# Regrouping the logit steps of the first attention in a two-layer encoder

## The chip, the core and the metric

The kernel runs on one core of a Trainium2 chip. A core has five engines that take their instructions from queues of their own, in order: TensorE (PE in the profile, with its weight loads as PEld), VectorE (DVE), ScalarE (ACT), GpSimd (POOL) and SyncE (SP, which here starts the transfers). Matmul results land in PSUM, from which VectorE and ScalarE read them into SBUF. The metric is the device time of one execution in microseconds (us), lower is better. The time before is a median of three runs.

## The reference

A sequence of 512 tokens of width 1024 goes through two layers. Each layer has a token mixer and, beside it, an attention of four heads into 256 memory tokens; their outputs are joined, projected and added to the stream, and a gated MLP with a short convolution follows. The change lies in the first layer, whose token mixer is the differential attention: six heads, each with two sets of queries and keys of 64 columns (`m` = 0, 1) and one set of values of 128 columns. Cut to what matters:

```python
q = rms_norm(q, qk_norm_g[0]) * (d ** -0.5)          # d = 64
k = rms_norm(k, qk_norm_g[1])
# for each block of 128 queries:
logits = einsum('bhmqd,bhmkd->bhmqk', qb, k) + bias  # two sets of logits a head
logits = where(key_chunk <= query_chunk, logits, -inf)
p = softmax(logits)
w = p[:, :, 0] - lam * p[:, :, 1]
o = rms_norm(einsum('bhqk,bhkv->bhqv', w, v), out_norm_g) * (1.0 - lam_init)

# memory attention, 4 heads of 64 columns:
o_mem = softmax(rms_norm(q_mem) * 64 ** -0.5 @ rms_norm(k_mem).T) @ v_mem

x = x + concatenate([o, o_mem]) @ w_out
x = x + conv_ffn(rms_norm(x), ...)
```

## The kernel before

**Matmuls of weights.** Weights and activations are split into a high and a low part (ScalarE's copy at L253 and VectorE's subtraction at L256 for weights; L310 and L311, the function `split`, for activations), and each product is made of three matmuls, high by high, low by high and high by low: `gemm` (L330 to L332) for projections, `product` (L351 to L353) for the output projection. These are full matmuls: 128 rows, 512 columns.

**The first attention.** The blocks of queries of a pair of heads are worked off in five steps. `TOGETHER` says which blocks (head, block) share a step, so that each step has up to 512 columns of keys:

```python
TOGETHER = (((0, 2), (0, 0)), ((0, 3),), ((0, 1), (1, 1)), ((1, 2), (1, 0)), ((1, 3),))
```

Three pairs of heads give steps 0 to 14. A step passes through three functions. `logits(t)` issues 6, 4, 8, 6 or 4 matmuls (for the five steps of a pair; the trace shows each as two, 12, 8, 16, 12 and 8), whose keys and queries have 64 rows only; the two sets `m` go to the upper and the lower half of the array and to two PSUM banks. VectorE then adds the bias and takes the row's extreme (L726), ScalarE takes the exponential (L729), and VectorE forms the weights `w`. `turn(t)` transposes them into a bank "tp" (L220), which ScalarE copies out (L748). `values(t)` multiplies them by the values into a bank "sm"; after the last block of a head, `output` squares the result on ScalarE (L771), `scale` normalises it on VectorE (L777, L779), and `finish` transposes it through a bank "tp" and splits it with L310 and L311. `prepare(h)` makes the queries and keys of a head: eight transposes through both banks "tp", each emptied by ScalarE (L682).

The memory attention has the same structure: `queries` (two banks "tp", L582), `logits` of a block of 128 queries (L591; 64 rows as well), `softmax` (L599 and L605 to L607 on VectorE, L603 on ScalarE), `turn` and `values`. The method `logits` takes any number of blocks: the first uses the banks "lg", a second one "tp" in the first layer and "sm" in the second, where two blocks are issued together. The memory's keys and values are made in `operands` and `keys` (L310, L551, L552, L560).

**PSUM.** There are four tags, "mm", "lg", "sm" and "tp", of two banks each (`bank`, L193). Banks of a tag are used in turn: who asks for one waits until its last reader is through.

**Order.** TensorE's order is that of the program (`manual_schedule`); the order of the other engines is the scheduler's. Through the first attention the program is read from a string, `SCRIPT`, by `do` (L633). A letter with a number calls a function, by the table `doing`: `L` is logits, `M` logits with the banks "tp" (in the table, but not used by this script), `T` turn, `V` values, `P` prepare, `N` the norms of queries and keys, `F` finish, `s` scale, `a` and `b` the memory operands of the two layers, `k` memory keys, `q` the memory queries (`q0` their norm, `q1` their transposes), `l`, `t`, `v` logits, turn and values of the memory attention, `X` the loads of the residual stream, `O` the last part of the output projection. A plain number is filler, in us by the program's own reckoning: `Filler.fill` takes full matmuls of the projections from a queue (six at a time for 512 columns) or of the output projection (three at a time, reckoned at 0.65) until the number is used up. In the trace the script's stretch lies between about 48 and 217 us.

The residual update (L1061, in `update`) reads the output projection's banks, "mm" among them, on VectorE.

Of the kernel before, what the change touches and what calls it, by code (L numbers as in the profile page):

```python
# [37 lines left out]

SCRIPT = """
    17.75 P0 3.9  # L40
    L0 a3 P1 8.45 a0 0.97
    L1 1.94 a1 T0
    L2 3.57 a2
    L3 T1 4.86 N2 V0 T2 N3 V1 12.33
    L4 P2 6.17 V2 T3
    L5 s0 T4 2.27 V3
    L6 P3 b1 V4 5.2 T5
    L7 T6 F0 7.14 b0
    L8 V5 T7 8.42 V6 s1 N5 N4 F1
    L9 V7 P4 b2 4.45 T8 T9 s2 3.0  # L50
    L10 V8 3.55 X P5 q0
    L11 b3 V9 T10 4.2
    L12 F2 V10 s3 T11 3.8 q1 k0
    L13 3.15 l0 V11 T12 3.65
    L14 F3 t0 3.3 V12 T13 t1 l1 3.9 T14 l2 t2 2.3 O k1 t3 s4 l3 v0 t4 V13 V14 t6 t5 1.3 t7 F4 v1 s5 F5 6.15 ! 4.55
"""

ORDER = (('v', 0), ('qk', 1), ('kv', 0), ('qk', 2), ('vm', 2), ('kv', 1))
# [28 lines left out]
def _pieces():  # L87

    plan = []

    def piece(key, name, i, ks, *ranges):
        plan.append((key, name, i, ks, ranges))

    for l in range(2):
        if l == 0:
            w = "w_in_diff"
            piece(("qk", 0), w, 0, K8, (0, 256), (768, 1024))
            for key in ORDER:
                if key[0] == "qk":
                    p = key[1]  # L100
                    piece(key, w, 0, K8, (256 * p, 256 * p + 256), (768 + 256 * p, 1024 + 256 * p))
                elif key[0] == "kv":
                    piece(key, "w_mem_kv", key[1], K8, (0, 512))
                elif key[0] == "vm":
                    p = key[1]
                    piece(key, w, 0, K8, (1536 + 256 * p, 1792 + 256 * p), (2304, 2560))
                else:
                    p = key[1]
                    piece(key, w, 0, K8, (1536 + 256 * p, 2048 + 256 * p))
        else:  # L110
            w = "w_in_gla"
            piece(("gm", 1), w, 0, K8, (2304, 2576))
            for c in range(5):
                piece(("g", c), w, 0, K8, (512 * c, min(512 * c + 512, 2304)))
        for i, part in enumerate(PASS[l]):
            for c, ks in part:
                piece(("o", l, i, c), "w_out", l, ks, (256 * c, 256 * c + 256))
        base = 0
        for nq in HALVES:
            for q in range(base, base + nq):  # L120
                piece(("ua", l, q), "w_up", l, K8, (256 * q, 256 * q + 256))
                piece(("ug", l, q), "w_up", l, K8, (DFF + 256 * q, DFF + 256 * q + 256))
            for c in range(4):
                piece(("dn", l, base, c), "w_down", l, tuple(range(2 * base, 2 * base + 2 * nq)),
                      (256 * c, 256 * c + 256))
            base += nq
    return plan


def _blocks():  # L130

    out = []
    for key, name, i, ks, ranges in _pieces():
        w = sum(b - a for a, b in ranges)
        step = WTILE // w
        out.append([(name, i, ks[j:j + step], ranges, w) for j in range(0, len(ks), step)])
    return out
# [42 lines left out]
def trunk(ctx, tc, head_d, x_t, mem_t, wpack, cols_a_d, cols_d, conv_d, gate_d, rel_bias, diff_lambda, consts, onehot, out):  # L180
# [12 lines left out]
    def bank(tag):  # L193
        return ps.tile([128, 512], F32, name=f"ps_{tag}", tag=tag)

    def xtile():
        return xs.tile([128, S], F32, name="xt", tag="xs", bufs=XS)
# [9 lines left out]
    def blk(b, w=128):  # L207
        return slice(w * b, w * b + w)
# [40 lines left out]
    plan, blocks, made = _pieces(), _blocks(), []  # L249
# [318 lines left out]
    class MemAttn:  # L568
# [13 lines left out]
                A.activation(self.qT[hp], p, AF.Copy, scale=c_mq(self.l))  # L582


        def logits(self, *blocks):
            banks = [(bank(tag), bank(tag)) for _, tag in zip(blocks, ("lg", "sm") if self.l else ("lg", "tp"))]
            for b, pl in zip(blocks, banks):
                for hp in range(2):
                    for j in range(2):
                        hh = blk(j, 64)  # L590
                        mm(pl[j][:, blk(hp, 256)], self.qT[hp][hh, blk(b)], kmT[self.l][hh, hp], start=True, stop=True)  # L591
            for b, pl in zip(blocks, banks):
                self.softmax(b, pl)
# [51 lines left out]
    def diff_layer(pool, mix, acc):  # L645
# [45 lines left out]
        def members(t):  # L691
            pr, s = divmod(t, len(TOGETHER))
            out, at = [], 0
            for j, i in TOGETHER[s]:
                out.append((2 * pr + j, i, 4 * j + i, at))
                at += 128 * (i + 1)
            return pr, out, at

        def bias(h):
            bt = heads[h]["bt"] = pool.tile([128, S], F32, name="bt", bufs=2)  # L700
            src = bass.AP(tensor=bias_d.tensor, offset=bias_d[h].offset + 1, ap=[[1, 128], [1, 512]])
            nc.sync.dma_start(bt, src)
            G.memset(bt[0:64, 0:64], -1e30)

        def logits(t, tag="lg"):
            pr, group, _ = members(t)
            P = pairs[pr]
            s2, nm, rc = P["s2"], P["nm"], P["rc"]
            for h, _, _, _ in group:
                if "bt" not in heads[h]:  # L710
                    bias(h)
            pls = bank(tag), bank(tag)
            for h, i, _, at in group:
                nk = 128 * (i + 1)
                cuts = (0, nk) if i == 0 else (0, nk // 2, nk)
                for k0, k1 in zip(cuts, cuts[1:]):
                    for m in range(2):
                        hh = blk(m, 64)
                        mm(pls[m][:, at + k0:at + k1], heads[h]["q"][hh, blk(i)], heads[h]["k"][hh, k0:k1],
                           start=True, stop=True)  # L720
            e = xtile(), xtile()
            for m in range(2):
                for h, i, g, at in group:
                    c = slice(at, at + 128 * (i + 1))
                    n1 = nm[:, 8 * m + g:8 * m + g + 1]
                    V.tensor_tensor_reduce(  # L726
                        out=e[m][:, c], in0=pls[m][:, c], in1=heads[h]["bt"][:, 127 + 128 * i::-1], scale=-1.0,
                        scalar=1e38, op0=ALU.add, op1=ALU.min, accum_out=n1)
                    A.activation(e[m][:, c], e[m][:, c], AF.Exp, scale=-1.0, bias=n1,  # L729
                                              accum_out=s2[:, m, g:g + 1])  # L730
            ids = sorted(g for _, _, g, _ in group)
            step = max(ids[-1] - ids[0], 1)
            b, lr = slice(ids[0], ids[-1] + 1, step), slice(8 + ids[0], 9 + ids[-1], step)
            V.reciprocal(rc[:, b], s2[:, 1, b])
            V.scalar_tensor_tensor(rc[:, lr], rc[:, b], nlam, s2[:, 0, b], op0=ALU.mult, op1=ALU.mult)
            for _, i, g, at in group:
                c = slice(at, at + 128 * (i + 1))
                V.scalar_tensor_tensor(e[1][:, c], e[1][:, c], rc[:, 8 + g:9 + g], e[0][:, c],
                                                    op0=ALU.mult, op1=ALU.add)
            live[t] = e[1]  # L740
# [57 lines left out]
        ma = MemAttn(pool, 0, qm, mix, False)  # L798
        ops, keys = [None] * 2, [None] * 2
        for key in ORDER:  # L800
# [16 lines left out]

        doing = {
            "L": logits, "M": lambda i: logits(i, "tp"), "T": turn, "V": values, "P": prepare, "F": finish,
            "N": lambda i: norms(i // 2, i % 2), "a": lambda i: ops[0]((2 * i, 2 * i + 1)),  # L820
            "b": lambda i: ops[1]((2 * i, 2 * i + 1)), "k": lambda i: keys[i]("sm"),
            "q": lambda i: ma.queries() if i else (F.need("v2"), ma.norm()),
            "l": lambda i: ma.logits(i), "t": ma.turn, "v": lambda i: ma.values(i, "sm"),
            "s": lambda i: scales.pop(i)(), "X": lambda i: load_x(x_t),
            "O": lambda i: last.append(out_proj(0, mix, 1, acc, 5)), "!": lambda i: F.flush()}
        do(SCRIPT, doing)
# [228 lines left out]
    def load_x(src):  # L1055
        for k in range(KT):
            xT[k] = xtile()
            nc.sync.dma_start(xT[k], src[k])
# [117 lines left out]
    for l in range(2):  # L1176
        with tc.tile_pool(name=f"at{l}", bufs=2) as pool:
            mix = [None] * 8
            sums, acc = acc, [None]
            if l == 0:  # L1180
                diff_layer(pool, mix, acc)
            else:
                gla_layer(pool, mix, sums)
                out_proj(1, mix, len(PASS[1]) - 1, acc)
                F.flush()
        with tc.tile_pool(name=f"ff{l}", bufs=2) as pool:
            acc = ffn(pool, l, acc)
# [73 lines left out]
```

## Time and profile before

| | us |
|---|---|
| time, median of 3 runs | 1168.63 (1167.96 to 1169.76) |
| time of the profiled execution | 1168.01 |
| span of the profiled execution | 1166.2 |
| PE busy | 1160.7 (100%) |
| PEld busy | 965.3 (83%) |
| DVE busy | 750.9 (64%) |
| ACT busy | 545.5 (47%) |
| POOL busy | 5.0 (0%) |

The span runs from the first to the last instruction that the profiler recorded; the time of the execution also takes in what lies around it. Busy times of different engines overlap. An engine that is busy all the time can still be shortened, since a matmul that waits for the array to change its shape counts as busy. The throttle granted TensorE its full clock (1.0) in this execution.

### The profile page before, as it was taken

To read this page: it belongs to the slowest core of one execution; us is meant where nothing else is said; L and a number is where in the kernel's file an instruction comes from. 1 tells how busy PE (TensorE), PEld (TensorE's weight loads), DVE (VectorE), ACT (ScalarE), POOL (GpSimd) and SP (SyncE) were. 2 spreads that over 40 slices of the span, in tenths; PEclk is the share of its full clock that TensorE was granted. 3 is DMA by queue.
4 is the path that set the end of the run, shared out by engine and by line. 5 is a ranking of instruction groups with operands and counts; after the bars stand their busy time and mean duration, and the time that the engine had idled before them with its cause. 6 is when DMAs were issued, how large, how long until landed. Compare 5 with 4: busy or idle time off the path is not lost.

```text
span 1166.2 us, 14790 instructions
## 1 busy us (share of the span) xinstructions
PE 1160.7 (100%) x5658; PEld 965.3 (83%) x5658; DVE 750.9 (64%) x1256; ACT 545.5 (47%) x951; POOL 5.0 (0%) x27
## 2 busy tenths in 40 slices
PE   9999999999999999999999999999999999999998
PEld 7888888888888888888888888988888888888887
DVE  7576778688677326677447637777876743576741
ACT  6676687555344213344437634436643421343420
POOL 0000000000000000000000000000000000000000
PEclk9999999999999999999999999999999999999999
DMA  8423242123223223222342230333232323232231
GB/s 295 158 70 99 78 141 73 63 103 130 85 90 120 83 88 124 75 91 98 120 148 68 81 108 3 110 121 109 93 123 73 98 102 108 85 114 73 89 101 45
DMA packets 39556, 117.68 MB, mean 101 GB/s; under 512 B 4703, under 2 KB 7192, under 8 KB 39486
## 3 DMA queue, kind: packets, MB, share of 16 engines
q1 hardware_dynamic: 39054, 116.35, 29.5%
q8 instruction: 44, 0.72, 0.3%
q10 hardware_dynamic: 432, 0.39, 0.1%
q14 instruction: 26, 0.21, 0.1%
HBM read 112.52 MB, written 4.21 MB: 100 GB/s over the span
## 4 chain that ended last, share of the span: by engine, by line
PE 98%; ACT 1%; DVE 1%; issue 0%; POOL 0%; DVEq 0%; POOLq 0%
PE ps_mm L352 9%; PE ps_mm L351 9%; PE ps_mm L353 9%; PE ps_sm L353 8%; PE ps_sm L352 8%; PE ps_sm L351 7%; PE ps_mm L330 6%; PE ps_mm L332 6%; PE ps_mm L331 6%; PE ps_tp L353 3%; PE ps_lg L353 3%; PE ps_lg L352 3%; PE ps_tp L352 3%; PE ps_lg L351 3%; PE ps_tp L351 3%; PE ps_tp L220 3%
## 5 line engine op out<-in xcount | busy, mean ns | idle before, releaser
L253 ACT CAST whi<-raw 128x1024 fp32r<-128x1024 f32 (+4 forms) x212 | 207.6, 986 | 245.4 <-PE ps_tp L352 120.9
L256 DVE TENSOR_TENSOR wlo<-raw,whi 128x1024 fp32r<-128x1024 f32 (+4 forms) x212 | 240.3, 1140 | 117.5 <-ACT whi L253 116.6
L351 PE MATMUL ps_mm<-xsh,whi 128*128 128x512 f32 x438 | 171.6, 392 | 0.0
L352 PE MATMUL ps_mm<-xsl,whi 128*128 128x512 f32 x438 | 170.6, 389 | 0.0
L353 PE MATMUL ps_mm<-xsh,wlo 128*128 128x512 f32 x438 | 170.5, 389 | 0.0
L351 PE MATMUL ps_sm<-xsh,whi 128*128 128x512 f32 x378 | 147.0, 389 | 0.0
L352 PE MATMUL ps_sm<-xsl,whi 128*128 128x512 f32 x378 | 147.0, 389 | 0.0
L353 PE MATMUL ps_sm<-xsh,wlo 128*128 128x512 f32 x378 | 147.0, 389 | 0.0
L330 PE MATMUL ps_mm<-whi,xsh 128*128 128x512 f32 (+2 forms) x336 | 129.1, 384 | 0.0
L332 PE MATMUL ps_mm<-whi,xsl 128*128 128x512 f32 (+2 forms) x336 | 126.1, 375 | 0.0
L331 PE MATMUL ps_mm<-wlo,xsh 128*128 128x512 f32 (+2 forms) x336 | 125.9, 375 | 0.0
L1113 ACT ACTIVATE cvo<-u,cv 128x512 f32<-128x512 f32 x88 | 71.4, 815 | 112.1 <-DVE u L1111 112.1
L352 PEld LDWEIGHTS ps_mm<-xsl,whi 128*128 128x128 f32 x438 | 82.3, 188 | 17.2 <-DVE xsl L311 0.4
L351 PEld LDWEIGHTS ps_mm<-xsh,whi 128*128 128x128 f32 x438 | 82.2, 188 | 17.1 <-issue 0.3
L353 PEld LDWEIGHTS ps_mm<-xsh,wlo 128*128 128x128 f32 x438 | 82.2, 188 | 17.1
L1114 DVE SCALAR_TENSOR_TENSOR cvo<-u,cv,cvo 128x512 f32<-128x512 f32 x88 | 65.7, 749 | 36.2 <-ACT cvo L1113 36.0
L352 PEld LDWEIGHTS ps_sm<-xsl,whi 128*128 128x128 f32 x378 | 70.9, 188 | 14.8
L351 PEld LDWEIGHTS ps_sm<-xsh,whi 128*128 128x128 f32 x378 | 70.9, 188 | 14.7
L353 PEld LDWEIGHTS ps_sm<-xsh,wlo 128*128 128x128 f32 x378 | 70.9, 188 | 14.7
L332 PEld LDWEIGHTS ps_mm<-whi,xsl 128*128 128x128 f32 x336 | 63.2, 188 | 11.6
L330 PEld LDWEIGHTS ps_mm<-whi,xsh 128*128 128x128 f32 x336 | 63.2, 188 | 11.3 <-ACT ks L659 0.3
L331 PEld LDWEIGHTS ps_mm<-wlo,xsh 128*128 128x128 f32 x336 | 63.3, 188 | 10.4
(295 smaller groups left out, 1760.1 us busy)
## 6 DMA issues: line engine op xcount, KB each, us to landing
raw<-in_wpack_dram SPq DMA_DIRECT2D x178, 512.0 KB, 3.5
xt<-in_x_t_dram SPq DMA_DIRECT2D x15, 256.0 KB, 5.2
raw<-in_wpack_dram SPq DMA_DIRECT2D x15, 256.0 KB, 3.0
raw<-in_wpack_dram SPq DMA_DIRECT2D x8, 384.0 KB, 3.0
xres<-xt SPq DMA_DIRECT2D x8, 256.0 KB, 3.0
xt<-xres SPq DMA_DIRECT2D x8, 256.0 KB, 5.4
out_dram<-xt SPq DMA_DIRECT2D x7, 256.0 KB, 2.0
bt<-bias_d SPq DMA_DIRECT2D x6, 256.0 KB, 4.1
```

The lines of the kernel that those rows point to most:

```text
L220: nc.tensor.transpose(dst, src, ident[:n, :n])
L253: ins = A.copy(hi[:, c], raw[:, c])
L256: V.tensor_sub(lo[:, c], raw[:, c], hi[:, c].bitcast(F32))
L330: mm(p, sh[k][:, blk(b)], hi, start=k == 0, stop=False)
L331: mm(p, sh[k][:, blk(b)], lo, start=False, stop=False)
L332: mm(p, sl[k][:, blk(b)], hi, start=False, stop=k == KT - 1)
L351: mm(p, hi[:, blk(n)], bh, start=i == first, stop=False)
L352: mm(p, hi[:, blk(n)], bl, start=False, stop=False)
L353: mm(p, lo[:, blk(n)], bh, start=False, stop=i == last)
L1113: A.activation(c, u[:, 2:], AF.Identity, scale=cv[l][:, 2, j:j + 1], bias=cv[l][:, 3, j:j + 1])
L1114: V.scalar_tensor_tensor(c, u[:, 1:S + 1], cv[l][:, 1, j:j + 1], c, op0=ALU.mult, op1=ALU.add)
```

## The change

The script is written anew from `L0` to `F5`; the second half of a neighbouring pair of steps is issued with `M`, directly behind the first. Runs of logits that stand together are then `L0 M1`, `L2 M3`, `L4`, `L5 M6`, `L7 M8`, `L9`, `L10 M11`, `L12 M13`, `L14 m0`, `l1` (now blocks 1 and 2) and `l3`, eleven where there were nineteen (fifteen of `L`, four of `l`). For that, the memory attention's `logits` can be told its banks, `l1` stands for two blocks, and a new letter `m` issues a block with the banks "tp". Turns, values, `prepare`, `finish` and the memory queries are regrouped around the joined steps: `P1` follows `L0 M1`, `P3` comes before `V2`, `T3` and `T4` before `L5`, `V8` and `P5` after `L10 M11`, and `q0` and `T10` directly after `P5`. The total of the filler stays, but it is cut up differently; between `t5` and `t7`, 1.3 becomes 0.65. The order of SyncE's and GpSimd's instructions stays the same.

```diff
 SCRIPT = """
     17.75 P0 3.9
-    L0 a3 P1 8.45 a0 0.97
-    L1 1.94 a1 T0
-    L2 3.57 a2
-    L3 T1 4.86 N2 V0 T2 N3 V1 12.33
-    L4 P2 6.17 V2 T3
-    L5 s0 T4 2.27 V3
-    L6 P3 b1 V4 5.2 T5
-    L7 T6 F0 7.14 b0
-    L8 V5 T7 8.42 V6 s1 N5 N4 F1
+    L0 M1 a3 3.4 P1 5.05 a0 0.97
+    1.94 a1 T0
+    L2 M3 a2 3.57
+    T1 4.86 N2 V0 T2 N3 V1 12.33
+    L4 P2 3.9 P3 2.27 V2 T3 2.27 T4
+    L5 M6 s0 V3 b1 2.6 V4 2.6 T5
+    L7 M8 3.5 T6 F0 3.64 b0
+    V5 T7 8.42 V6 s1 N5 N4 F1
     L9 V7 P4 b2 4.45 T8 T9 s2 3.0
-    L10 V8 3.55 X P5 q0
-    L11 b3 V9 T10 4.2
-    L12 F2 V10 s3 T11 3.8 q1 k0
-    L13 3.15 l0 V11 T12 3.65
-    L14 F3 t0 3.3 V12 T13 t1 l1 3.9 T14 l2 t2 2.3 O k1 t3 s4 l3 v0 t4 V13 V14 t6 t5 1.3 t7 F4 v1 s5 F5 6.15 ! 4.55
+    L10 M11 V8 4.85 X b3 V9 P5 q0 T10 2.9
+    F2 V10 s3 T11 2.5
+    L12 M13 3.9 q1 k0
+    0.65 V11 T12 3.65
+    L14 m0 3.9 F3 V12 T13 0.65 t0 0.65 t1 0.65 l1 3.25 T14 t2 1.3 O k1 t3 s4 l3 v0 t4 V13 V14 t6 t5 0.65 t7 F4 v1 s5 F5 6.15 ! 4.55
 """
...
-        def logits(self, *blocks):
-            banks = [(bank(tag), bank(tag)) for _, tag in zip(blocks, ("lg", "sm") if self.l else ("lg", "tp"))]
+        def logits(self, *blocks, tags=None):
+            banks = [(bank(tag), bank(tag)) for _, tag in zip(blocks, tags or (("lg", "sm") if self.l else ("lg", "tp")))]
             for b, pl in zip(blocks, banks):
                 for hp in range(2):
                     for j in range(2):
...
-            "l": lambda i: ma.logits(i), "t": ma.turn, "v": lambda i: ma.values(i, "sm"),
+            "l": lambda i: ma.logits(*((1, 2) if i == 1 else (i,))), "m": lambda i: ma.logits(i, tags=("tp",)),
+            "t": ma.turn, "v": lambda i: ma.values(i, "sm"),
```

## The prediction

> **What bounds the kernel now.** I read the page's span and its chain that ended last, then the stage of the change (48 to 217 us) as one window, then the timelines of TensorE, ScalarE and VectorE inside it.
>
> ```profile
> span 1166.2 us, 14790 instructions
> ...
> PE 98%; ACT 1%; DVE 1%; issue 0%; POOL 0%; DVEq 0%; POOLq 0%
> ```
>
> The window (columns: stretch, length, busy time and instructions of PE, PEld, DVE, ACT and POOL, granted clock, DMA share, GB/s):
>
> ```profile
> 48.00:217.00 169.00, 169.00 (x1042) 139.86 (x1041) 126.29 (x335) 124.50 (x340) 0.58 (x4) 1.00 0.29 94
> ```
>
> TensorE makes up 98% of the chain; in the stage it never idles, at full granted clock, while VectorE and ScalarE have 169.00 − 126.29 = 42.7 and 44.5 us free. So a microsecond taken out of TensorE's stream is worth a microsecond, and a wait put into it costs one. The stage's instructions on TensorE are the same in both kernels; only their order differs. The sum is therefore: what switching between kinds of matmul saves, less the waits that the new order makes.
>
> **What joining saves.** TensorE rows (start, length, operation, shape, count) of a step of logits standing alone in the filler, and of two blocks of memory logits issued in one run by the second layer:
>
> ```profile
> 64.38 0.39 PE L331 MATMUL ps_mm<-wlo,xsh 128*128 128x512 f32 x1
> 64.61 0.39 PE L332 MATMUL ps_mm<-whi,xsl 128*128 128x512 f32 x1
> 64.93 1.14 PE L719 MATMUL ps_lg<-kT,qT 64*128 64x256 f32 x8
> 65.99 0.50 PE L330 MATMUL ps_mm<-whi,xsh 128*128 128x512 f32 x1
> 66.33 0.40 PE L331 MATMUL ps_mm<-wlo,xsh 128*128 128x512 f32 x1
> ...
> 637.69 0.39 PE L332 MATMUL ps_mm<-whi,xsl 128*128 128x512 f32 x1
> 638.01 1.14 PE L591 MATMUL ps_lg<-kmT,xt 64*128 64x256 f32 x8
> 638.98 1.03 PE L591 MATMUL ps_sm<-kmT,xt 64*128 64x256 f32 x8
> 639.93 0.50 PE L330 MATMUL ps_mm<-whi,xsh 128*128 128x512 f32 x1
> 640.28 0.40 PE L331 MATMUL ps_mm<-wlo,xsh 128*128 128x512 f32 x1
> ```
>
> Full matmuls start 64.61 − 64.38 = 0.23 apart. Into the 64-row logits it takes 0.32, and the first full matmul afterwards also holds 0.34. One run of eight logits lies in 66.33 − 64.61 = 1.72, of which two full matmuls are 0.45: it adds 1.27. Sixteen in one run lie in 640.28 − 637.69 = 2.59 and add 2.13. Two single runs would add 2.54, so a join is worth 2.54 − 2.13 = 0.40. Nineteen runs become eleven: 8 × 0.40 = 3.2. The filler is cut into more stretches (about 30 for 23, counted in the script); most of the new cuts are at transposes, not logits. A cut costs at most the 0.34 − 0.23 = 0.11 seen after logits, at least nothing; I take 0.03, nearer to nothing, since both sides of it are 128-row matmuls: 7 × 0.03 = 0.2. Joins: 3.0 (2.4 to 3.2).
>
> **What the joined steps wait for.** The second of a pair takes both "tp" banks, which transposes use too. So T3 and T4 come before L5M6, and M6 needs T4's copy gone; M8 needs T5's. Rows of one such turn (T5, L7, T6 and VectorE's last read of L7's logits):
>
> ```profile
> 120.84 0.60 PE L220 MATMUL ps_tp<-C,xt 128*128 128x128 f32 x4
> 121.36 1.16 PE L719 MATMUL ps_lg<-kT,qT 64*128 64x128 f32 x16
> 122.46 0.66 PE L220 MATMUL ps_tp<-C,xt 128*128 128x128 f32 x4
> ...
> 124.29 0.42 DVE L726 CUSTOM_DVE_ANT_0 xt<-ps_lg,bt 128x256 f32<-128x256 f32 x1
> ```
>
> T5 takes 0.52, L7 about 1.0. T5's copy ends early enough if ScalarE is free; one weight split (0.96) begun as the transposes end makes it 0.52 + 0.96 + 0.58 = 2.06 against 1.52, a wait of 0.54. Between 0 and 0.54 I take the middle, 0.25, for each of M6 and M8, since no row of before says where the split will fall. M3 waits in the same way for T0, whose copy can be done at 0.64 + 0.58 = 1.22, as in the rows at 68.85 and 69.49 below; 0.3 to spare, so nothing, up to 0.54 with a split. M1 has banks long free; M11 comes 3.0 of filler after T9, M13 2.5 after T11, and these get nothing; without that cover each would cost up to 0.54 too.
>
> A page of the Trainium skill speaks against the change: "TensorEngine Tiling (Array Packing)", section Performance Considerations, says that tiling speeds TensorE but not PSUM evacuation, so the PSUM copy may become the bottleneck. In the rows above TensorE went on 1.10 after L7's first matmul while VectorE read its logits until 124.71, so reading out is already slower than issuing. By that rule the joins would only move the wait, and the sum would be 1172.6 in place of 1169.6 (rival S). But the reading ends long before the next pair, L9, which the script puts more than 15 us of filler after L7M8. I go by the rows.
>
> **T10 and V10.** P5 (eight transposes, both "tp" banks) now stands after V9, and T10 follows with no filler: it waits for ScalarE to empty P5's first bank. V10 then waits for T10's copy.
>
> ```profile
> 68.85 0.60 PE L220 MATMUL ps_tp<-C,xt 128*128 128x128 f32 x4
> ...
> 160.72 0.60 PE L220 MATMUL ps_tp<-C,qs 128*128 128x128 f32 x4
> 161.16 0.60 PE L220 MATMUL ps_tp<-C,ks 128*128 128x128 f32 x4
> ...
> 69.49 0.58 ACT L748 COPY xt<-ps_tp 128x512 f32<-128x512 f32 x1 [0.74 <-PE ps_tp L220]
> ...
> 161.63 0.67 ACT L682 ACTIVATE qT<-ps_tp,cols 128x512 f32<-128x512 f32 x1
> 162.20 0.68 ACT L682 ACTIVATE kT<-ps_tp,cols 128x512 f32<-128x512 f32 x1
> 162.77 1.15 ACT L386 ACTIVATE xt<-qm 128x512 f32<-128x512 f32 x2
> ...
> 164.51 0.51 ACT L310 ACTIVATE xsh<-xt,cols_a 128x256 fp32r<-128x256 f32 x1
> 164.91 0.30 ACT L241 ACTIVATE rs_y<-ss,eps 128x16 f32<-128x16 f32 x1
> ...
> 166.32 0.36 ACT L771 ACTIVATE xt<-ps_sm,rs 128x128 f32<-128x128 f32 x1
> ...
> 167.69 0.59 ACT L748 COPY xt<-ps_tp 128x512 f32<-128x512 f32 x1
> ```
>
> From a group of transposes to its copy: 69.49 − 68.85 = 0.64. Then qT 0.67 and 0.05 to release: 1.36. TensorE is there after 2 × 0.44 = 0.87 (161.16 − 160.72). T10 waits 0.49 (0.76 if the copy starts as late as in the row at 161.63).
>
> On ScalarE, T10's copy stands behind qT and kT (2 × 0.57), b3's two L310 (2 × 0.40), V9's four L771 (167.69 − 166.32 = 1.37), q0's two L386 (1.15, less 0.1 of overlap) and L241, L242 (0.3): 4.65. It starts 0.64 + 4.65 = 5.29 after P5 and is through at 5.92. TensorE arrives at 0.87 + 0.49 + 0.36 (T10) + 2.84 (filler 2.9) + 0.44 (F2) = 5.0. V10 waits 0.92. Below, 0.3, if L386 or L310 fall behind the copy; above 1.4 with a split (0.96) half in front.
>
> **L12M13 to T12.** Two steps of softmax and both memory evacuations now come within 9 us. ScalarE and VectorE rows of these operations:
>
> ```profile
> 170.05 0.51 ACT L729 ACTIVATE xt<-xt,nmd 128x256 f32<-128x256 f32 x1 [0.62 <-DVE nmd L726]
> ...
> 172.03 0.67 ACT L310 ACTIVATE xsh<-ps_tp,cols 128x512 fp32r<-128x512 f32 x1
> ...
> 175.62 1.05 ACT L253 CAST whi<-raw 128x1024 fp32r<-128x1024 f32 x1 [0.53 <-PE ps_mm L332]
> 176.58 1.26 ACT L582 ACTIVATE xt<-ps_tp,cols 128x512 f32<-128x512 f32 x2
> ...
> 180.59 0.39 ACT L253 CAST whi<-raw 128x256 fp32r<-128x256 f32 x1
> ...
> 181.61 0.62 ACT L386 ACTIVATE xt<-xt 128x512 f32<-128x512 f32 x1
> ...
> 174.19 1.90 DVE L256 TENSOR_TENSOR wlo<-raw,whi 128x768 fp32r<-128x768 f32 x2
> ```
>
> T12 needs a bank that q1 filled, hence L582. From L12's start: a split of 1024 columns (0.96) from 0.1, its L256 on VectorE (1.90/2 = 0.95), so that L726 begins at 2.0; its first part 0.47; L12's four L729 172.03 − 170.05 = 1.98, M13's as much; a split 0.96, a small split with L551 and L552 181.61 − 180.59 = 1.02, L386 0.52, L582 0.63 and 0.05: 9.6. TensorE: L12 1.0, M13 0.97, eighteen full matmuls 4.2, q1 0.88, k0 0.36, three full 0.79, V11 0.89: 9.1. T12 waits 0.55 (0 to 1.5: another split before it).
>
> **Output projection and tail.** m0 and the doubled l1 put softmax ahead of L1061, which empties a "mm" bank.
>
> ```profile
> 195.97 1.29 DVE L599 TENSOR_REDUCE nmm<-ps_lg 128x2 f32<-128x512 f32 x2 [0.67 <-PE ps_lg L591]
> ...
> 196.69 0.47 ACT L603 ACTIVATE xt<-ps_lg,nmm 128x256 f32<-128x256 f32 x1 [0.35 <-DVE nmm L599]
> ...
> 214.99 0.69 DVE L779 TENSOR_TENSOR o<-ps_sm,rs 128x512 f32<-128x512 f32 x1
> 215.59 0.74 DVE L311 SCALAR_TENSOR_TENSOR xsl<-ps_tp,cols,xsh 128x512 fp32r<-128x512 f32 x1
> ...
> 216.41 0.66 PE L220 MATMUL ps_tp<-C,o 128*128 128x128 f32 x4
> ```
>
> l1's matmuls take 639.93 − 638.01 = 1.92 and 0.11; TensorE needs the bank twelve full matmuls (12 × 0.227 = 2.72) later, at 4.76. L599 starts about 1.1 after l1, L603 0.72 after it, six L603 of 0.45 come before VectorE's L605, then L1061 0.68: 5.2 to 5.4. Wait 0.6 (0 to 1.2: three L603 less or more). At m0 half of the same backlog: 0.25 (0 to 0.6).
>
> At the tail, o5 (L779) is written by 214.99 + 0.69 = 215.68 and F5 starts at 216.41: 0.73 to spare. Half the filler between t5 and t7 goes (three matmuls, 0.68), and F4's L311 moves ahead of L779 (0.67). t5 waits 0.1, F4 0.2 for t5's copy, which gives 0.3 of slack back: F5 waits 0.68 + 0.67 − 0.73 − 0.3 = 0.32, to 0.5 as L779 may also stand behind a split's L256. Tail 0.7 (0 to 1.4).
>
> **What moves at no cost.** P3 moves between P2 and V2; its second bank needs P2's kT: 0.64 + 2 × 0.57 = 1.78 against 3.9 of filler, so 2.1 of ScalarE backlog is covered, two splits; a third would cost 0.96. V3, V4, V8, T6, F0 move by a few us behind copies that had already that slack. SyncE's and GpSimd's orders stay: X's loads, the bias loads and memsets (first member of each pair) keep their sequence, and the weights' loads follow the same filler. A load that came late would hold ScalarE's split and the copies behind it for as long; none is issued later than before.
>
> **Sum.** Waits 0.25 + 0.25 + 0.49 + 0.92 + 0.55 + 0.25 + 0.6 + 0.7 = 4.0 (1.2 to 7). Less 3.0 of joins: +1.0. The profiled execution took 1168.01 (span 1166.2 and 1.8 around it), so 1169.0; it lies 0.62 under the median of the runs, 1168.63, against which I predict 1169.6. The likeliest case's own range, waits 2.5 to 5.3 against 3.0, is 1168.1 to 1170.9.
>
> **Rivals.** Measurable here is 0.2%, or 2.3 us.
> - A, faster: the joins pay 3.2 and the scheduler's order on ScalarE gives the copies way, so only T10's 0.49 stays: −2.7, 1165.9. For it: 44.5 us of ScalarE free in the stage, and T10 has the only wait that needs no backlog. Against it: a queue is in order, and the copies come behind what was issued earlier. 0.12.
> - C: T10, V10 and 0.3 elsewhere: 1.7 less 3.0, −1.3, 1167.3. 0.15.
> - B, slower: ScalarE's and VectorE's backlog from L12M13 to T12. The slack there is used up, so each further us of it is a us of TensorE. One more split (0.96) and one more step's four L726 (0.42 each, at 124.29) ahead of L582 make 2.3 after overlaps: 1171.9. It decides from 1.4 more. For it: ScalarE has its idle time elsewhere, not in this stretch. 0.18.
> - S: reading out PSUM limits every joined run, and the joins give nothing: +4.0, 1172.6. For it: the 124.71 row; against it: 2.59 for two blocks in the second layer with TensorE not waiting. 0.06.
>
> Forecast 0.49. Faster is A, 0.12; same is C and the forecast, 0.64; slower is B and S, 0.24. The range 1166.3 to 1172.2 leaves out A's middle and most of S and B's end.
>
> **What would show it.** Right: joined logit runs of 16 to 28 matmuls followed by one 0.34, eleven runs in all; holes on TensorE ahead of T10, V10, T12 and the projection after l1, put down to ScalarE and VectorE. Wrong: the holes missing (A, C), a hole above 1.5 ahead of T12 (B), or holes inside the joined runs, ahead of M's first matmul (S).

## The result, and the profile after

The changed kernel takes 1170.35 us (median of 22 runs, 1169.6 to 1172.26) against 1168.63 in the same comparison: a ratio of 1.0014, with a 95% interval of 1.0008 to 1.002. It is slower by 1.7 us. 1169.6 was forecast, a loss of 1.0, with 1166.3 to 1172.2 as the range. Its script is one line shorter, so down to the table `doing` its line numbers are lower by one (L330 is L329, L719 is L718); L1061 is still L1061.

From the page of the changed kernel, the span and the chain that ended last:

```profile
span 1168.1 us, 14779 instructions
...
PE 96%; ACT 2%; DVE 1%; DMA 0%; issue 0%; SPq 0%; DVEq 0%
```

The span grew by 1.9 and TensorE's share of the chain fell from 98% to 96%. The waits of TensorE between 48 and 219 us (what it waited for, us in total, times, longest); the same view of the kernel before has no row there:

```profile
PE ps_sm L759 <- ACT xt L747: 0.7, 1, 0.7
PE ps_mm L350 <- DVE xt L1061: 0.6, 1, 0.6
PE ps_tp L219 <- DVE o L778: 0.4, 1, 0.4
PE ps_tp L219 <- ACT qT L681: 0.3, 1, 0.3
PE ps_tp L219 <- ACT xt L581: 0.2, 1, 0.2
```

These are V10, the output projection behind l1, F5, T10 and T12, five of the places named in the prediction. The view counts less than a wait costs (V10's 0.7 is 0.89 from start to start). So in what follows a hole is the distance from one start to the next, less the same distance where nothing is waited for. TensorE's timeline of the changed kernel, ahead of and behind each hole:

```profile
53.33 1.14 PE L718 MATMUL ps_lg<-kT,qT 64*128 64x192 f32 x12
54.30 1.03 PE L718 MATMUL ps_tp<-kT,qT 64*128 64x256 f32 x8
...
110.27 1.22 PE L718 MATMUL ps_tp<-kT,qT 64*128 64x256 f32 x8
111.41 1.16 PE L759 MATMUL ps_sm<-vv,xt 128*128 128x128 f32 x8
...
121.69 1.39 PE L718 MATMUL ps_tp<-kT,qT 64*128 64x192 f32 x12
123.01 0.50 PE L329 MATMUL ps_mm<-whi,xsh 128*128 128x512 f32 x1
...
162.31 1.05 PE L759 MATMUL ps_sm<-vv,xt 128*128 128x128 f32 x8
163.20 0.60 PE L219 MATMUL ps_tp<-C,qs 128*128 128x128 f32 x4
163.64 0.60 PE L219 MATMUL ps_tp<-C,ks 128*128 128x128 f32 x4
164.58 0.66 PE L219 MATMUL ps_tp<-C,xt 128*128 128x128 f32 x4 [0.34 <-ACT qT L681]
...
167.82 0.60 PE L219 MATMUL ps_tp<-C,o 128*128 128x128 f32 x4
169.15 1.16 PE L759 MATMUL ps_sm<-v,xt 128*128 128x128 f32 x8 [0.73 <-ACT xt L747]
170.14 0.60 PE L219 MATMUL ps_tp<-C,xt 128*128 128x128 f32 x4
...
181.65 1.05 PE L759 MATMUL ps_sm<-v,xt 128*128 128x128 f32 x8
182.94 0.66 PE L219 MATMUL ps_tp<-C,xt 128*128 128x128 f32 x4 [0.24 <-ACT xt L581]
...
202.83 0.39 PE L352 MATMUL ps_mm<-xsh,wlo 128*128 128x512 f32 x1
203.85 0.50 PE L350 MATMUL ps_mm<-xsh,whi 128*128 128x512 f32 x1 [0.64 <-DVE xt L1061]
...
215.95 1.97 PE L628 MATMUL ps_sm<-xt,vm 128*64 128x128 f32 x32
218.34 0.63 PE L219 MATMUL ps_tp<-C,o 128*128 128x128 f32 x4 [0.42 <-DVE o L778]
```

L0 M1 (53.33, 54.30) run through: 0.97 a step, and 0.105 between the last matmul of one and the first of the next, as within a step. Behind the joined steps M6 takes 111.41 − 110.27 = 1.15 where 0.96 is free of waits, M8 123.01 − 121.69 = 1.32 for 0.97. T10 starts 0.94 after P5's second half in place of 0.44, V10 1.33 after F2 in place of 0.44, T12 1.29 after V11 in place of 0.89. Behind l1 two matmuls start 203.85 − 202.83 = 1.02 apart in place of 0.23, and the next (204.19) 0.34 later. v1 lasts 218.34 − 215.95 = 2.39 to F5, where it was 216.41 − 214.51 = 1.90.

From here on the measure is the stretch from P0's first transpose to F5's, which holds the same instructions of TensorE in every kernel here: before 216.41 − 48.22 = 168.18, after 218.34 − 48.27 = 170.07, so +1.89. (Differences are taken before rounding, so the last digit of one can be off by one from the rows shown.) It is steadier than a single execution's time, since the second layer adds waits that come and go: the profiled execution of the first experiment has 1.2 us there in one wait, that of the changed kernel none.

### The profile page after: what moved, and what is told of

It reads as the page before. It is cut to its first block, busy times and chain, and to the rows that moved or that the text cites. A ratio compares the mean times of both kernels' runs of the same rounds, so it can differ in the third digit from the quotient of the medians.

```text
span 1168.1 us, 14779 instructions
## 1 busy us (share of the span) xinstructions
PE 1160.1 (99%) x5658; PEld 965.4 (83%) x5658; DVE 750.6 (64%) x1256; ACT 545.1 (47%) x951; POOL 5.0 (0%) x27
## 4 chain that ended last, share of the span: by engine, by line
PE 96%; ACT 2%; DVE 1%; DMA 0%; issue 0%; SPq 0%; DVEq 0%
PE ps_mm L350 9%; PE ps_mm L351 9%; PE ps_mm L352 9%; PE ps_sm L352 7%; PE ps_sm L350 7%; PE ps_sm L351 7%; PE ps_mm L329 6%; PE ps_mm L331 6%; PE ps_mm L330 6%; PE ps_tp L352 3%; PE ps_lg L352 3%; PE ps_lg L350 3%; PE ps_tp L350 3%; PE ps_tp L351 3%; PE ps_lg L351 3%; PE ps_tp L219 2%
## 5 line engine op out<-in xcount | busy, mean ns | idle before, releaser
L255 DVE TENSOR_TENSOR wlo<-raw,whi 128x1024 fp32r<-128x1024 f32 (+4 forms) x212 | 240.3, 1139 | 121.2 <-ACT whi L252 120.3
L329 PE MATMUL ps_mm<-whi,xsh 128*128 128x512 f32 (+2 forms) x336 | 129.5, 385 | 0.0
L330 PE MATMUL ps_mm<-wlo,xsh 128*128 128x512 f32 (+2 forms) x336 | 126.0, 375 | 0.0
L329 PEld LDWEIGHTS ps_mm<-whi,xsh 128*128 128x128 f32 x336 | 63.2, 188 | 11.4 <-issue 0.7
L330 PEld LDWEIGHTS ps_mm<-wlo,xsh 128*128 128x128 f32 x336 | 63.3, 188 | 10.3
```

Source lines behind the costliest of these rows:

```text
L255: V.tensor_sub(lo[:, c], raw[:, c], hi[:, c].bitcast(F32))
L329: mm(p, sh[k][:, blk(b)], hi, start=k == 0, stop=False)
L330: mm(p, sh[k][:, blk(b)], lo, start=False, stop=False)
```

## The experiments

The theory (W): joins gain, and the loss is a handful of waits, each for one copy or reading in a queue behind other work. Rivals: the backlog of ScalarE and VectorE has no slack, so that waits only move (B); reading PSUM out makes the joins worth nothing (S); the finer cutting of the filler costs the time (G).

**T10 away from P5, filler taken from behind T11.**

```diff
-    L10 M11 V8 4.85 X b3 V9 P5 q0 T10 2.9
-    F2 V10 s3 T11 2.5
+    L10 M11 V8 4.85 X b3 V9 P5 q0 1.3 T10 2.9
+    F2 V10 s3 T11 1.2
```

> Of the changed kernel only the order behind P5 is altered: six full matmuls (the script's 1.3) are put between P5 and T10 and taken from behind T11. Theory W (the loss is a few waits for copies on ScalarE): in the changed kernel T10 waits 0.50 and V10 0.89, with 0.15 of slower starts behind them; both go, the span falls by 1.2 to 1.5 from 1168.1 to about 1166.7, with no new wait above 0.3. Theory B (ScalarE's backlog has no slack from here to T12, so that a wait taken away at one place comes back at the next): V11's end and T12 take over, T12's wait of 0.40 grows by 0.8 or more and the span falls by less than 0.6. Theory G (the loss is the filler's finer cutting): no fall, since the number of cuts grows by one.

The time was 1170.09 (ratio to before 1.001, 1.0 to 1.0019), the stretch 169.71: only 0.36 less. T10 no longer waits and V10 hardly does (0.03), but three later places do. TensorE's timeline:

```profile
172.91 1.16 PE L718 MATMUL ps_lg<-kT,qT 64*128 64x128 f32 x16
174.38 1.21 PE L718 MATMUL ps_tp<-kT,qT 64*128 64x192 f32 x12 [0.32 <-ACT xt L747]
...
181.78 1.05 PE L759 MATMUL ps_sm<-v,xt 128*128 128x128 f32 x8
183.49 0.66 PE L219 MATMUL ps_tp<-C,xt 128*128 128x128 f32 x4 [0.66 <-ACT xt L581]
```

L12 takes 1.48 for 1.00 to M13, which waits for T11's copy; M13 takes 0.17 more; V11 to T12 1.71 for 0.89. That is 0.48 + 0.17 + 0.42 = 1.1 given back. It was what B had foretold, but it could also be the filler that had been taken away behind T11. The next run tells these apart.

**T10 away from P5, filler taken from ahead of b3.**

```diff
-    L10 M11 V8 4.85 X b3 V9 P5 q0 T10 2.9
+    L10 M11 V8 3.55 X b3 V9 P5 q0 1.3 T10 2.9
```

> Of the changed kernel only the order behind P5 is altered, as in the run before it that put six full matmuls between P5 and T10, but they now come from the filler ahead of b3 and V9, so the filler of 2.5 behind T11 stays whole. In that earlier run T10 (0.50) and V10 (0.89) no longer waited, but the stretch from P0 to F5 fell by only 0.36, since L12 waited 0.50, M13 0.17 and T12 0.42 more. Theory W2 (those new waits came from the filler that was taken away behind T11: T11's copy and a weight split were no longer covered): here they stay away, T12's wait stays at 0.40, and the stretch falls by 1.3 to 1.5, from 170.07 to about 168.7. Theory B (ScalarE's and VectorE's backlog up to T12 takes up whatever TensorE gains): T12's wait grows by 1.0 or more and the stretch falls by less than 0.5.

The stretch was 168.65, 1.42 less, in the middle of what W2 says; one run took 1168.8. The same places:

```profile
172.55 1.16 PE L718 MATMUL ps_lg<-kT,qT 64*128 64x128 f32 x16
173.54 1.04 PE L718 MATMUL ps_tp<-kT,qT 64*128 64x192 f32 x12
...
180.75 1.05 PE L759 MATMUL ps_sm<-v,xt 128*128 128x128 f32 x8
182.04 0.66 PE L219 MATMUL ps_tp<-C,xt 128*128 128x128 f32 x4 [0.24 <-ACT xt L581]
```

L12 takes 0.99 and V11 to T12 1.29, as in the changed kernel. B falls: the queues have room if the filler stands where the copy is waited for. The first run's loss came from its own edit.

**T4 and T5 earlier.**

```diff
-    L4 P2 3.9 P3 2.27 V2 T3 2.27 T4
-    L5 M6 s0 V3 b1 2.6 V4 2.6 T5
+    L4 P2 3.9 P3 2.27 V2 T3 0.97 T4 1.3
+    L5 M6 s0 V3 b1 2.6 V4 1.3 T5 1.3
```

> Of the changed kernel only T4 and T5 are moved: 1.3 of the script's filler now lies between each and the joined logits L5 M6 and L7 M8; the joined runs themselves are as they were. Theory W: the holes of 0.19 inside L5 M6 and 0.35 inside L7 M8 are waits for the transposed weights' copies out of the banks tp, so both are gone and the span falls by 0.5 to 1167.6. Theory S (reading PSUM out limits joined runs): the holes belong to the joined runs and stay, and the span stays within 0.15 of 1168.1.

```profile
121.50 1.04 PE L718 MATMUL ps_tp<-kT,qT 64*128 64x192 f32 x12
122.47 0.50 PE L329 MATMUL ps_mm<-whi,xsh 128*128 128x512 f32 x1
```

M8 now takes 0.97, M6 0.96: the holes are gone though each pair's logits are read from the same banks by the same instructions. S falls for these holes. The stretch was 169.71, 0.36 less, not 0.5. The rest is a new wait at F0, behind T6:

```profile
125.33 0.60 PE L219 MATMUL ps_tp<-C,xt 128*128 128x128 f32 x4
125.91 0.63 PE L219 MATMUL ps_tp<-C,o 128*128 128x128 f32 x4
```

F0 starts 0.58 after T6 where it was 0.43 in the changed kernel, and its own matmuls take 0.03 more. It needs the second bank of M8, whose logits VectorE reads with L725, eight almost in a row from 122.83 behind a split's L255; the last runs from 125.49 to 125.76. So 0.18 of the 0.53 moved to a wait for reading out. In the changed kernel ScalarE's rows show why M8 waited:

```profile
120.36 1.05 ACT L252 CAST whi<-raw 128x1024 fp32r<-128x1024 f32 x1 [0.53 <-PE ps_mm L331]
121.31 0.58 ACT L747 COPY xt<-ps_tp 128x512 f32<-128x512 f32 x1
```

A weight split begun 0.2 after T5 (120.16) stands ahead of T5's copy, which ends at 121.89.

**V13 behind l1, and filler back between t5 and t7.**

```diff
-    ... l1 3.25 T14 t2 1.3 O k1 t3 s4 l3 v0 t4 V13 V14 t6 t5 0.65 t7 ...
+    ... l1 2.6 V13 0.65 T14 t2 0.65 O k1 t3 s4 l3 v0 t4 V14 t6 t5 1.3 t7 ...
```

> Of the changed kernel only the stretch behind l1 is altered: V13 is moved from behind t4 to behind the first 2.6 of filler after the doubled l1, and 0.65 of filler goes back between t5 and t7. Theory W: the output projection's wait for its bank (0.80 and 0.11 of slower start) is covered by V13's 0.9, F5's wait for o5 (0.49) by the filler, t5's 0.12 stays or goes: the span falls by 1.2 to 1.6, to about 1166.7. Theory B: the same ScalarE and VectorE work still has to be done ahead of F5, so half of it or more comes back as a longer wait at T14, t2 or F5, and the span falls by less than 0.7.

The time was 1169.44 (ratio 1.0005, 0.9996 to 1.0015), the stretch 169.43, 0.64 less. The holes behind l1 and ahead of F5 closed, but a new wait came, in the view of waits between 48 and 219 us:

```profile
PE ps_tp L219 <- DVE xt L615: 0.8, 1, 0.8
```

t5 waits for t4's copy (L615), 1.0 from start to start; V13 had covered it. The number is B's, the cause is not a general backlog but one cover used twice.

**l1 taken apart again.** In the table, `l` is again as before the change.

```diff
-    ... t0 0.65 t1 0.65 l1 3.25 T14 t2 1.3 O ... t6 t5 0.65 t7 ...
+    ... t0 0.65 t1 l1 2.6 T14 l2 t2 1.65 O ... t6 t5 1.3 t7 ...
```

> Of the changed kernel only the end is altered: l1 is taken apart into l1 and l2 as in the kernel before, l1 follows t1 directly, and the filler between t5 and t7 is 1.3 again (2.6 of filler behind l1, 1.65 behind t2). Theory W: the output projection's hole behind l1 (0.91) and F5's (0.49), t5's and F4's (0.2) go, one join (0.35 to 0.4) is lost: the stretch from P0 to F5 falls by 1.0 to 1.3, from 170.07 to about 168.9. Rival (that join pays more than its waits cost, the waits being backlog that comes back elsewhere): the stretch falls by less than 0.4 or rises.

The stretch was 168.78, 1.29 less; one run took 1169.1. The edit does two things, which the timeline keeps apart: 0.57 comes from l1 taken apart (its hole of 0.91 gone, 0.34 of the join lost), 0.72 from the tail, where the filler between t5 and t7 closes F5's and F4's holes. So at this place the join in l1 costs more than it gains.

**Less filler ahead of T12.**

```diff
-    0.65 V11 T12 3.65
+    V11 T12 4.3
```

> Of the changed kernel only one thing is altered: the three full matmuls between k0 and V11 are put behind T12, so TensorE comes to T12 about 0.68 earlier. Theory W, with its statement that the slack ahead of T12 is used up: T12's wait grows from 0.40 to between 1.0 and 1.1, one for one, and the span rises by 0.6 to 1168.7, unless the later stretch had waits that the shift shortens (the wait behind L14 and m0 stays, 0.27). Rival: T12 waits for a transfer or a fixed step before it and not for a queue's order; then its wait grows too but the span stays within 0.2, since the filler put behind T12 shortens the later waits.

The stretch was 170.76, 0.69 more, and V11 to T12 took 1.99 (180.85 to 182.84 in the timeline), a wait of 1.10 for 0.40. One run took 1170.93. TensorE came 0.70 earlier and waited 0.70 longer: T12 has no slack and pays one for one.

**All waits mended at once.** The edits for T10 (second form) and for T4 and T5 together, `l` in the table as before the change, and:

```diff
-    0.65 V11 T12 3.65
-    L14 m0 3.9 F3 V12 T13 0.65 t0 0.65 t1 0.65 l1 3.25 T14 t2 1.3 O ... t5 0.65 t7 ...
+    1.3 V11 T12 3.0
+    L14 m0 2.6 F3 V12 0.65 T13 t0 0.65 t1 l1 3.25 T14 l2 t2 2.3 O ... t5 1.3 t7 ...
```

> The changed kernel with its waits mended: 1.3 of filler between P5 and T10 (taken from ahead of b3), between T4 and L5 M6, and between T5 and L7 M8; 0.65 more ahead of V11 and T12; the block pair l1 taken apart again into l1 and l2 as before the change, with the filler between t5 and t7 back at 1.3 and 2.6 in place of 3.9 behind L14 m0. Seven of the eight joins stay. Theory W: with no wait left over 0.3 the joins show: the first stretch (P0 to F5) falls from 170.07 to 166.0 to 166.6, which is 1.6 to 2.2 below the kernel before (168.18), and the time is 1166.4 to 1167.0 against 1168.6. Theory B: backlog makes new waits as fast as old ones go, and the stretch stays above 168. Theory S: the joins themselves are worth nothing, and with all waits gone the stretch is that of before, 168.0 to 168.4.

The time was 1168.12 (ratio 0.9996, 0.9987 to 1.0005), the stretch 167.76: 0.4 under the kernel before, not 1.6 to 2.2. The view of waits between 48 and 218 us has one row:

```profile
PE ps_tp L219 <- DVE xsl L310: 0.9, 1, 0.9
```

t0 waited 1.08 from start to start for L310 of F3, which I had moved next to it; F0 (0.18, behind T6) and a filler matmul behind L12 M13 (0.31) waited too. These three are 1.6.

**The pairs apart again, in the mended order.** One unit of filler between the members of each of the seven pairs (as L0 1.3 M1 in place of L0 M1), taken from behind them.

> The mended kernel with its seven joined runs taken apart: one unit of filler (six full matmuls, three for m0) is put between the first and second member of each pair and taken from the filler behind the pair; all else, banks and order of turns too, is as in the mended kernel. Theory W: a join is worth 0.35 to 0.40, so the stretch from P0 to F5 is 2.5 to 2.8 longer than the mended kernel's, in holes of the shape 0.09, 0.10, 0.10 and 0.11 around each member, and the time 1168.9 to 1169.6. Theory S: the same stretch within 0.5.

The time was 1174.03 (ratio 1.0046, 1.0033 to 1.0059), the stretch 173.75, 6.0 more than mended, not 2.5 to 2.8. About half is not the joins but two waits that the shorter filler behind M8 and M13 made, in the view of waits between 48 and 223 us:

```profile
PE ps_tp L219 <- DVE nmd L725: 2.9, 2, 2.1
```

The price of a join alone stands where nothing waits: from P0 to T1, with two pairs (L0 and M1, L2 and M3) and 158 records of TensorE, equal in kind in all three kernels. P0, T1 and, of the first two, the first full matmul behind T1, of before, after, and apart:

```profile
48.22 0.60 PE L220 MATMUL ps_tp<-C,qs 128*128 128x128 f32 x4
...
75.83 0.66 PE L220 MATMUL ps_tp<-C,xt 128*128 128x128 f32 x4
76.25 0.48 PE L330 MATMUL ps_mm<-whi,xsh 128*128 128x512 f32 x1
```

```profile
48.27 0.60 PE L219 MATMUL ps_tp<-C,qs 128*128 128x128 f32 x4
...
75.26 0.60 PE L219 MATMUL ps_tp<-C,xt 128*128 128x128 f32 x4
75.62 0.49 PE L329 MATMUL ps_mm<-whi,xsh 128*128 128x512 f32 x1
```

```profile
48.36 0.60 PE L219 MATMUL ps_tp<-C,qs 128*128 128x128 f32 x4
...
76.23 0.60 PE L219 MATMUL ps_tp<-C,xt 128*128 128x128 f32 x4
```

To T1's start that is 27.61, 27.00 and 27.87. But T1 itself is slower where it stands behind L3's logits, as in the kernel before (0.41 for 0.35). To the first full matmul behind it, which starts at 76.59 in the kernel taken apart, it is 28.02, 27.35 and 28.23. So two joins saved 0.67 in the change, 0.34 each; where filler stands between the members they are worth 0.88, 0.44 each. To T1's start it was 27.00 in all nine kernels that have this part of the changed script.

**Mended again.**

```diff
-    L7 M8 3.5 T6 F0 3.64 b0
+    L7 M8 4.8 T6 F0 2.34 b0
...
-    L12 M13 3.9 q1 k0
-    1.3 V11 T12 3.0
-    L14 m0 2.6 F3 V12 0.65 T13 t0 0.65 t1 l1 3.25 T14 l2 t2 2.3 O ...
+    L12 M13 3.9 V11 q1 k0
+    1.3 T12 3.0
+    L14 m0 2.6 F3 V12 0.65 T13 1.3 t0 0.65 t1 l1 2.6 T14 l2 t2 1.65 O ...
```

> The mended kernel with its own remaining holes closed: T6 and F0 come after 4.8 of filler behind L7 M8 in place of 3.5 (T6 waited 0.15 more for M8's banks to be read), V11 stands ahead of q1 (a filler matmul waited 0.31 for L1061 behind L12 M13's softmax), and 1.3 of filler in place of nothing lies between T13 and t0 (t0 waited 1.08 for VectorE's L310 of F3). Theory W: these 1.5 go, and the stretch from P0 to F5 falls from 167.76 to 166.1 to 166.5, 1.7 to 2.1 under the kernel before (168.18); time 1166.5 to 1167.2 against 1168.6. Theory B (the backlog on ScalarE and VectorE fills any gain): the stretch stays above 167.3. Theory S (joins worth nothing): it ends at 168 or above.

```profile
span 1164.4 us, 14785 instructions
```

P0 and F5 in its timeline:

```profile
48.13 0.60 PE L219 MATMUL ps_tp<-C,qs 128*128 128x128 f32 x4
...
214.69 0.66 PE L219 MATMUL ps_tp<-C,o 128*128 128x128 f32 x4
```

The time was 1166.94 against 1168.51 (ratio 0.9988, 0.9979 to 0.9997): faster than both kernels. The stretch is 214.69 − 48.13 = 166.55, 1.63 under before, just short of what W gave; 0.30 is still lost at T7 behind V5, a hole that this order made: T6, moved to a later place, left its copy behind three weight splits on ScalarE (127.13 to 129.96). The view of waits has no row in the stage.

## Why the prediction was right

Direction and mechanism held, and the time lay in the range; of the size the sum gave about half. It was −3.0 of joins and +4.0 of waits, +1.0; measured in the stretch are about +4.4 of waits and +1.9 in all, which leaves −2.5 for the joins.

- **The waits**, predicted and measured: M6 0.25, 0.18; M8 0.25, 0.35; T10 0.49, 0.50; V10 0.92, 0.89; T12 0.55, 0.40; the projection behind m0 0.25, 0.27; behind l1 0.6, 0.91; the tail 0.7, 0.67 (F5 0.49, F4 0.18, t5 none). Sum 4.0, 4.2; slower starts behind T10, V10 and T12 add 0.2. No other hole over 0.1 came: P3, M1, M3, M11, M13, V3, V4 and V8 moved at no cost, as said. M6 and M8 owe their fit in part to luck: 0.25 was the middle of 0 to 0.54. T5's copy stood behind a weight split, as supposed, T4's behind L657 and L658 (109.01 to 109.72). The term for m0 was half of l1's and had no ledger of its own.
- **V10's ledger** held row by row. ScalarE's timeline of the changed kernel behind P5:

```profile
163.84 0.69 ACT L681 ACTIVATE qT<-ps_tp,cols 128x512 f32<-128x512 f32 x1 [1.33 <-PE ps_tp L219]
...
168.49 0.60 ACT L747 COPY xt<-ps_tp 128x512 f32<-128x512 f32 x1
```

  qT, kT, b3's two L309, V9's four L770 and q0's two L385 run without a gap, and the copy starts 168.49 − 163.20 = 5.29 after P5, the predicted figure. ScalarE, idle for a quarter of the stage, holds TensorE up by 0.89 here, because the copy stands at its place in the queue. The Trainium skill says so too ("PSUM — Partial Sum Buffer", section Engine vs sequencer instructions: the queues of ScalarE, VectorE and GpSimd are strict first in, first out), and these rows agree. Two of the other ledgers held nearly as well: for T12, L581 starts 182.21 − 173.45 = 8.76 after L12 (foretold 8.9); behind l1, L1061 starts 203.11 − 198.26 = 4.85 after l1 (foretold 4.5 to 4.7), which is most of the 0.3 that this term lacked.
- **The term that was mis-sized is "a join is worth 0.40"**. 0.40 came from runs with filler on both sides, and there it is right (0.44). But of the nineteen runs of before only four are followed by filler; nine are followed by transposes and six by values. P1 behind L0 before, and P1 in the filler after:

```profile
54.35 0.66 PE L220 MATMUL ps_tp<-C,qs 128*128 128x128 f32 x4
54.85 0.60 PE L220 MATMUL ps_tp<-C,ks 128*128 128x128 f32 x4
```

```profile
59.48 0.60 PE L219 MATMUL ps_tp<-C,qs 128*128 128x128 f32 x4
59.91 0.60 PE L219 MATMUL ps_tp<-C,ks 128*128 128x128 f32 x4
```

  Its first four transposes take 0.50 behind logits and 0.43 in filler: leaving the logits cost 0.07 there, not the 0.11 that filler pays. That and 0.03 for the cut bring 0.40 to 0.33; measured for the first two joins is 0.34. Over all eight the sum leaves 4.4 − 1.9 = 2.5, 0.31 each, in place of 3.0; the last 0.03 a join stays unexplained. So this term makes up 0.5 of the 0.9 by which the sum fell short; the waits make up the rest.
- **The rivals.** A and C fell with T10, V10 and l1 in the view of waits. B did not come in the change (T12 waited 0.40), though its condition is real: the run with less filler ahead of T12 paid one for one. S fell: M6's and M8's holes closed when T4 and T5 moved, though 0.18 came back at F0 as a wait for reading out, and the kernel mended again is faster than the one before. G fell: the second form of T10's mend has one cut more and saved 1.42.
- **The rule weighed in the prediction** ("TensorEngine Tiling (Array Packing)" of the Trainium skill, Performance Considerations) did not bind in the change; the page puts it for a speedup of four times. Nearest to it came F0 with T4 and T5 moved, which waited 0.18 behind eight L725 almost in a row. In the run with the pairs apart, with six full matmuls between M8 and T6, F0 waited 2.3 for the last L725 on M8's logits; but ahead of that one VectorE worked off L737 and a split's L255 (127.73 to 129.66), so this wait was again a place in a queue. The same page's Key Properties, in the section Tiling Modes, say that changing the tiling mode drains TensorE; the rows agree that the change costs time: 0.32 in place of 0.23 into the logits, 0.34 out of them, 0.105 between two joined steps. How much of the 0.34 is the drain is not shown, since the first full matmul behind transposes, which use 128 rows as well, holds 0.31 to 0.32.

## What to carry to other kernels

Price a regrouping by the neighbours it really has: a saved switch was worth 0.44 between filler and 0.34 where its neighbours were transposes. Walk each moved step's queue in order and compare the end of its copy with the engine's arrival, for that foretold every hole's place and most of the sizes to within about 0.3 us; an engine that idles for a quarter of the stage was still late at one spot. And when a wait is mended with filler, ask what that filler was covering: most of the mends here opened a new hole, of 0.2 to 1.1 us.

## What was not expected

After a hole the next group is slower too, by as much as after a change of kind: V10's eight matmuls took 170.14 − 169.15 = 0.99 for V9's 0.89 (163.20 − 162.31), and the matmul behind the wait at l1 0.34 for 0.23. The length of the hole does not matter much: in the second form of T10's mend V10 came only 0.04 late and took 0.99 all the same. In these places a wait cost 0.05 to 0.11 more than its length.

Where nothing waits, TensorE's stream is steadier than the runs' times by far: P0 to T1 was 27.00 in every kernel with that order, while runs of one kernel spread over 2.7 us.
